# A hybrid encoder layer on one core: first sweep, transposes of the decayed k and the decay inputs one product later, the decays' products directly ahead of those inside the chunk

## The chip, the cores and the metric

The kernel runs on one core of one Trainium2 chip. The metric is the device time of one execution in microseconds (us). The time before is 1314.11 us, the median of three runs (1314.02 to 1314.79).

## What is computed

One layer of an encoder for 2048 tokens of width 1024, in float32. One projection of the input makes the columns of two groups of heads; each group mixes the tokens in its own way; their outputs, put side by side, pass an output projection, and a LayerNorm over the scaled residual ends the layer. The change lies in the first group, gated linear attention in both directions (the reference cut to it):

```python
def gla_chunked(q, k, v, log_a, strict):
    b = jnp.cumsum(gc, axis=3)                 # running sum of the log decays in a chunk
    b_last = b[:, :, :, -1:, :]
    q_dec = qc * jnp.exp(b)
    k_dec = kc * jnp.exp(-b)
    k_tail = kc * jnp.exp(b_last - b)
    attn = jnp.where(mask, jnp.einsum('nbhtd,nbhsd->nbhts', q_dec, k_dec), 0.0)
    o_intra = jnp.einsum('nbhts,nbhsv->nbhtv', attn, vc)
    def step(state, inp):
        o = jnp.einsum('bhtd,bhdv->bhtv', qd, state)
        state = state * jnp.exp(bl)[..., None] + jnp.einsum('bhsd,bhsv->bhdv', kt, vv)
        return state, o

log_af = jax.nn.log_sigmoid(lr_f @ wg2_f + bg_f) / GLA_TAU     # lr: 16 columns of the projection
o = rms_norm(gla_chunked(q, k, v, log_af) + flip(gla_chunked(flip(q), flip(k), flip(v), flip(log_ab))))
```

The second group is latent attention with a softmax and rotary position tables (cos and sin of position times frequency). Those tables are computed by VectorE during the first sweep too, and for that reason they matter here.

## The kernel before, in words

Every large product is done in three matmuls (`mm3`, L420, L421, L422): each float32 operand is split into a rounded high part and a low rest, and high·high, low·high and high·low are added up. ScalarE writes the high part (`hi`, L366), and VectorE or GpSimd subtracts it to give the low one (`lo`, L372). So most tiles come as pairs: `xah`/`xal` (input), `kh`/`kl`, `qbh`/`qbl`, `kth`/`ktl`, `Ah`/`Al`.

The first sweep (`sweep_a`, L603) goes over 16 chunks of 128 tokens, from the last to the first: i = 0 to 15, chunk c = 15 - i. Steps 1 to 3 follow an order written out by hand (`ORDER_A`). Steps 4 to 15 are made by the callback `step(i, STEPS_A)`, with one period of about 22.5 us. In each, TensorE runs four groups of eight products over the model width: `ipa_0` (288 columns: q and the decay inputs lr), `ipa_1` (384: k and the first part of v), `ipa_2` (384: the rest of v) and the gate `ipg` (512). Between them stand the small products of the linear attention. `STEPS_A` says after which product of which group each stands; "cur" is for the step's own chunk, "prev" for the chunk before:

- after product 4 of `ipa_0`: transposes of q and k of the previous chunk (`qT`, `kT`), from which VectorE makes `qd` (L937) and `kd` (L956) with the decay factors E;
- after product 3 of `ipa_1`: `kt` (L970), four transposes of the decayed k of the previous chunk, and `lrT` (L870), one transpose of this chunk's decay inputs, which VectorE writes as `lr`. ScalarE copies them to `kth` and `lrTs`;
- after product 5 of `ipa_1`: `z` (L882), the decays' products, four matmuls from `lrTs`. With them come, in program order, ScalarE's Abs, Exp and Ln (L886, L888, L890) and VectorE's `za` (L892), two scans (L903, L905), the chunk sums `cl` and E (L915); `zdone` names the instruction of L915. `cw` (L925) is issued with `z`;
- after product 7 of `ipa_1`: `Ap` (`ga_intra`), the products inside the previous chunk. ScalarE copies one half to `At` (L987), VectorE fills the other in by a mask (L989), then `Ah` and `Al` (L372);
- after product 3 of `ipa_2`: `Up`, the state's products; then `Us` by VectorE (L1028) and four GpSimd instructions (L1030 on `Us`, L1036 and L1055 on `Sb`, L1051 on `Sm`);
- after product 3 of `ipg`: `Op`, then `oi` (L1008, L1010).

A group's results leave PSUM right after its last product, ahead of what `STEPS_A` puts there: ScalarE's `k` and high part of `VV` after `ipa_1`. After `ipg` the gate is made in `gs` by three ScalarE instructions and one of VectorE (`silu`, L1477 to L1483).

Two PSUM buffers serve `ipa_0`, `ipa_1`, `ipa_2` and `ipg` in turn, so a step's `ipa_1` writes where the `ipg` of the step before stood, and its first weight load waits until VectorE's `gs` (L1483) has read that. GpSimd also makes `xal` (L372, 128x1024), the low part of a later chunk's input, once ScalarE has written `xah`; `xah` waits for the last matmul that reads the buffer, in `ipg`.

The position tables' angles come in parts (`rope_angles`, L558 to L598), one part in each of the steps 4 to 8, ordered behind that step's `zdone`. Steps 5, 6 and 7 each have a rounding (L566 and L567) and three L570 instructions; step 5 has L580 too, and step 7 begins with L590.

Engines run their own instructions in the program's order, and a scheduler makes that order from dependencies and estimated times; so a later `z` also moves instructions of ScalarE and VectorE.

Of the kernel before, what the change touches and what calls it, by code (L numbers as in the profile page):

```python
# [56 lines left out]
av.2 av.2 gs.3 cw.3 gs.3  # L57
"""

STEPS_A = {(0, 4): [("q", "prev"), ("k", "prev")], (1, 3): [("kt", "prev"), ("lrT", "cur")],  # L60
           (1, 5): [("z", "cur"), ("cw", "cur")], (1, 7): [("intra", "prev")], (2, 3): [("state", "prev")],
           (3, 3): [("av", "prev")]}
ENGINES = tuple(getattr(mybir.EngineType, n) for n in ("PE", "Activation", "DVE", "Pool", "SP"))
LATE_ORDER = ENGINES[1], ENGINES[3], ENGINES[4]
RND = 1.5 * 2.0 ** 23
# [290 lines left out]
class K:  # L356
# [25 lines left out]
    def in_order(self, last, engines=None):  # L382
# [6 lines left out]
        for i in traced[n:]:  # L389
            if i.engine in (engines or ENGINES):  # L390
                if i.engine in last:
# [219 lines left out]
    def sweep_a(self):  # L611
        tc, nc, ins, cp = self.tc, self.nc, self.ins, self.cp
        with ExitStack() as ctx:
# [26 lines left out]
            with tc.tile_pool(name="sta", bufs=1, reuse_waits="tile") as sta:  # L640
# [5 lines left out]
                for g, (c0, n) in enumerate(A_GROUPS):  # L646
                    k = 0
# [30 lines left out]
            def step(i, steps):  # L678

                def after(g, k):  # L680
                    for n, d in steps.get((g, k), ()):
                        run(n, i if d == "cur" else i - 1)
                for g in range(3):
                    for k in self.products(ch[i], g, after):
                        pass
                    after(g, NK - 1)
                if i and ch[i]["c"] not in LATE_GATES:
                    for k in self.gate_products(ch[i]["c"], *ch[i]["x"], ip):
                        after(3, k)
                    self.gate_end(ch[i]["c"], g1)  # L690
# [9 lines left out]
            for t in ORDER_A.split():  # L700
                n, i = t.split(".")
# [6 lines left out]
            for i in range(4, NCH):  # L708
                c = ch[i]["c"]
                if c > 0:  # L710
                    for f in (self.ga_ld, self.ga_x):
                        for _ in f(i + 1):
                            pass
                else:
                    self.xlate = [self.split_x(xp, self.load_x(NCH - 1, "xb"), NCH - 1, "xb")]
                    self.xraw = self.load_x(NCH - 2, "xb")
                step(i, STEPS_A)
                if i < 4 + 5:
                    with self.after(ch[i]["zdone"]):
                        next(rope)  # L720
                if i == 9:
                    self.rope_tables(hpi)
            i = NCH - 1
# [335 lines left out]
    def late_gates(self):  # L1059
# [23 lines left out]
        with self.part("wz"):  # L1083
            self.Wz = next(wz)
        self.tail = {e: self.merge(e, names) for e, names in zip(ENGINES[1:], (TAIL_ACT, TAIL_DVE))}

# [922 lines left out]
```

## Time and profile before

| | |
|---|---|
| median of three runs | 1314.11 us (1314.02 to 1314.79) |
| the profiled execution's own time | 1313.98 us |
| its span in the profile | 1312.0 us |
| TensorE busy | 1288.9 us of the span (98%) |
| VectorE, ScalarE, GpSimd busy | 963.2, 812.9, 785.0 us |
| `kt` of step 4 and of step 15 start at | 91.73 and 339.49 us of the span |

In the profile's rows PE is TensorE's matmul, PEld its weight load (which may run beside the matmul ahead of it), DVE is VectorE, ACT ScalarE and POOL GpSimd. A row of the timeline has the start in us from the span's start, the duration in us, engine, line, operation, the tile written and the tiles read, sizes, and how many instructions of one kind were put together (x4). In brackets stands how long the engine was idle before it, and what ended that. Matmuls overlap, so what one costs is read from the distance between starts. A row of the waits has the waiting engine, tile and line, what it waited for, the sum in us, the times, and the longest.

### The profile page before, as it was taken

Reading aid. Unit: us, or ns where it says so; the run is one execution under the profiler, and the core shown is the slowest. Engines: PE = TensorE matmul, PEld = TensorE weight load, DVE = VectorE, ACT = ScalarE, POOL = GpSimd, SP = SyncE. Lnnn points to the kernel's source line nnn. Section 1 sums busy time; section 2 is a strip of 40 time slices with the busy share of each in tenths; the row PEclk is TensorE's granted clock in tenths of the full one; section 3 lists DMA queues with packets and bytes.
Section 4 is the critical chain, followed back from the end, with each engine's and each line's share of the span. In section 5 each row is a group of like instructions: output and inputs, shape, how many; then the busy total and the mean of one; then the engine's idle time right before and its main releaser. Section 6 shows DMA issues by size and latency. Waiting matters only on the chain.

```text
span 1312.0 us, 19984 instructions
## 1 busy us (share of the span) xinstructions
PE 1288.9 (98%) x7081; PEld 1130.2 (86%) x7081; DVE 963.2 (73%) x1712; ACT 812.9 (62%) x1339; POOL 785.0 (60%) x494
## 2 busy tenths in 40 slices
PE   7999999999999999999999999999999999999997
PEld 7999999999889999999788888888888887788886
DVE  7967685655675455555888888888888888469997
ACT  6765656555575656664787877888888888511110
POOL 0143333232467666671388888889999999764441
PEclk9999999999999999999999999999999999999999
DMA  8132313132475555655401111122223110576662
GB/s 283 63 99 55 92 53 93 49 80 66 152 245 173 193 192 177 204 198 184 114 1 41 41 42 41 41 57 64 58 70 101 48 41 9 89 234 200 216 193 97
DMA packets 107819, 145.81 MB, mean 111 GB/s; under 512 B 17250, under 2 KB 62694, under 8 KB 107720
## 3 DMA queue, kind: packets, MB, share of 16 engines
q1 hardware_dynamic: 99128, 142.41, 35.3%
q0 software_dynamic: 672, 2.10, 0.4%
q8 instruction: 56, 0.92, 0.3%
q10 hardware_dynamic: 7920, 0.03, 0.3%
q14 instruction: 43, 0.35, 0.2%
HBM read 94.14 MB, written 50.36 MB: 110 GB/s over the span
## 4 chain that ended last, share of the span: by engine, by line
PE 65%; ACT 2%; POOL 1%; DMA 1%; DVE 1%; issue 0%; SPq 0%; DVEq 0%; ACTq 0%; POOLq 0%
PE pS L1521 4%; PE pS L1524 4%; PE pS L1523 4%; PE pS L1525 4%; PE o L420 4%; PE pS L1522 4%; PE o L422 4%; PE o L421 4%; PE po L421 2%; PE po L422 2%; PE po L420 2%; PE pz L421 2%; PE pz L420 2%; PE pz L422 2%; PE ipm L422 2%; PE ipm L420 2%
## 5 line engine op out<-in xcount | busy, mean ns | idle before, releaser
L372 POOL TENSOR_TENSOR pl<-s,ph 128x1024 fp32r<-128x1024 f32 x128 | 306.8, 2411 | 67.0 <-ACT ph L366 61.8
L1543 DVE TENSOR_TENSOR rm<-pS,rm 128x512 f32<-128x512 f32 x210 | 144.9, 690 | 44.2 <-ACT s L1530 39.0
L1530 ACT ACTIVATE s<-pS 128x1024 f32<-128x1024 f32 x128 | 131.4, 1026 | 67.9 <-PE pS L1525 65.9
L1567 DVE TENSOR_TENSOR s<-s,mb 128x1024 f32<-128x1024 f32 x128 | 151.2, 1213 | 9.5 <-PE mb L1561 9.3
L1030 POOL TENSOR_TENSOR Us<-Us,cw 128x512 f32<-128x512 f32 x16 | 18.5, 1157 | 226.7 <-DVE Us L1028 174.9
L366 ACT ACTIVATE ph<-s 128x1024 fp32r<-128x1024 f32 x128 | 135.0, 1056 | 16.7 <-PE o L422 16.1
L1571 ACT ACTIVATE s<-s 128x1024 f32<-128x1024 f32 x128 | 131.4, 1050 | 13.8 <-DVE s L1567 13.7
L420 PE MATMUL ipa<-wah,xah 128*128 128x384 f32 (+1 forms) x384 | 130.9, 341 | 6.1 <-ACT wah L366 5.9
L422 PE MATMUL ipa<-wah,xal 128*128 128x384 f32 (+1 forms) x384 | 125.3, 326 | 0.0
L421 PE MATMUL ipa<-wal,xah 128*128 128x384 f32 (+1 forms) x384 | 124.9, 325 | 0.0
L1521 PE MATMUL pS<-qh,ckvT_h 128*128 128x512 f32 x256 | 103.7, 405 | 0.7 <-ACT s L1571 0.4
L420 PE MATMUL o<-ph,vh 128*128 128x512 f32 x256 | 102.6, 401 | 0.0
L422 PE MATMUL o<-ph,vl 128*128 128x512 f32 x256 | 101.3, 396 | 0.0
L1524 PE MATMUL pS<-rh,krs 128*128 128x512 f32 x256 | 101.2, 395 | 0.0
L421 PE MATMUL o<-pl,vh 128*128 128x512 f32 x256 | 101.1, 395 | 0.0
L1523 PE MATMUL pS<-qh,ckvT_l 128*128 128x512 f32 x256 | 100.9, 394 | 0.0
L1525 PE MATMUL pS<-rl,krs 128*128 128x512 f32 x256 | 100.7, 393 | 0.0
L1522 PE MATMUL pS<-ql,ckvT_h 128*128 128x512 f32 x256 | 100.6, 393 | 0.0
L1594 DVE TENSOR_TENSOR ap<-ap,s 128x512 f32<-128x512 f32 x120 | 83.1, 692 | 7.0 <-ACT s L1571 5.1
L372 POOL TENSOR_TENSOR ol<-of,oh 128x512 fp32r<-128x512 f32 x32 | 43.1, 1347 | 61.5 <-ACT oh L366 61.5
L420 PEld LDWEIGHTS ipa<-wah,xah 128*128 128x128 f32 x384 | 73.6, 192 | 7.2 <-ACT wah L366 6.4
L420 PE MATMUL pz<-xch,wzh 128*128 128x256 f32 x256 | 74.8, 292 | 0.0
(325 smaller groups left out, 3862.0 us busy)
## 6 DMA issues: line engine op xcount, KB each, us to landing
xcf<-xT_dram SPq DMA_DIRECT2D x16, 512.0 KB, 5.1
xr<-x_dram SPq DMA_DIRECT2D x16, 512.0 KB, 5.8
out_dram<-rr SPq DMA_DIRECT2D x32, 256.0 KB, 2.0
xaf<-xT_dram SPq DMA_DIRECT2D x14, 512.0 KB, 4.1
oib<-oi_s SPq DMA_DIRECT2D x16, 256.0 KB, 5.3
qdb<-qd_s SPq DMA_DIRECT2D x16, 256.0 KB, 4.4
SU<-su_s SPq DMA_DIRECT2D x16, 256.0 KB, 4.5
ub<-u_s SPq DMA_DIRECT2D x16, 256.0 KB, 4.8
```

What stands on the lines that cost most here:

```text
L366: return nc.scalar.activation(dst, src, AF.Copy).ins
L372: return e.tensor_tensor(dst, src, hi.bitcast(F32), ALU.subtract).ins
L420: mm(out, ah, bh, start=start, stop=False)
L421: mm(out, ah, bl, start=False, stop=False)
L422: mm(out, al, bh, start=False, stop=stop)
L1521: mm(ps[:, e], kh, qh, start=True, stop=False)
L1522: mm(ps[:, e], kh, ql, start=False, stop=False)
L1523: mm(ps[:, e], kl, qh, start=False, stop=False)
L1524: mm(ps[:, e], kr, rh, start=False, stop=False)
L1525: mm(ps[:, e], kr, rl, start=False, stop=True)
L1543: V.tensor_tensor(d["rm"], src[:, e], d["rm"], ALU.max)
L1567: V.tensor_tensor(s, s, d["mb"][:, None, :].to_broadcast([P, 2, QB]), ALU.subtract)
```

## The change

`kt` and `lrT` go from behind product 3 to behind product 4 of `ipa_1`; `z` and `cw` go from behind product 5 to behind product 7, directly ahead of `intra`. In the last step (c = 0) `z` and `cw` stay one product further ahead, behind product 6.

```diff
-STEPS_A = {(0, 4): [("q", "prev"), ("k", "prev")], (1, 3): [("kt", "prev"), ("lrT", "cur")],
-           (1, 5): [("z", "cur"), ("cw", "cur")], (1, 7): [("intra", "prev")], (2, 3): [("state", "prev")],
+STEPS_A = {(0, 4): [("q", "prev"), ("k", "prev")], (1, 4): [("kt", "prev"), ("lrT", "cur")],
+           (1, 7): [("z", "cur"), ("cw", "cur"), ("intra", "prev")], (2, 3): [("state", "prev")],
            (3, 3): [("av", "prev")]}
+STEPS_A_LAST = {**STEPS_A, (1, 6): [("z", "cur"), ("cw", "cur")], (1, 7): [("intra", "prev")]}
...
-                step(i, STEPS_A)
+                step(i, STEPS_A if c else STEPS_A_LAST)
```

One line more makes every line behind L62 higher by one in the changed kernel.

**Step 5, TensorE.** The rows around the moved products, before; `wah_206` stands for product 3 of `ipa_1`, `wah_208` for product 4, and so on to `wah_214` for product 7:

```order
L422 MATMUL ipa_1_1479<-wah_206,xal_1185 128x384
L970 MATMUL kt_1492<-ident,kd_1459 128x128 x4
L870 MATMUL lrT_1501<-ident,lr_221 98x128
L420 MATMUL ipa_1_1479<-wah_208,xah_1184 128x384
...
L422 MATMUL ipa_1_1479<-wah_210,xal_1185 128x384
L882 MATMUL z_1511<-lrTs_1503,wg 128x128 x4
L420 MATMUL ipa_1_1479<-wah_212,xah_1184 128x384
...
L422 MATMUL ipa_1_1479<-wah_214,xal_1185 128x384
L420 MATMUL Ap_1546<-qbh_222,kh_1461 128x256
```

And now:

```order
L423 MATMUL ipa_1_1479<-wah_208,xal_1185 128x384
L971 MATMUL kt_1495<-ident,kd_1459 128x128 x4
L871 MATMUL lrT_1504<-ident,lr_221 98x128
L421 MATMUL ipa_1_1479<-wah_210,xah_1184 128x384
...
L423 MATMUL ipa_1_1479<-wah_214,xal_1185 128x384
L883 MATMUL z_1522<-lrTs_1506,wg 128x128 x4
L421 MATMUL Ap_1546<-qbh_222,kh_1461 128x256
```

`kt` and `lrT` have moved by one product, `z` by two, and nine matmuls instead of six stand between `lrT` and `z`. It is the same in steps 4 to 9 and 11 to 14. In step 10, where the scheduler puts `lrT` and `z` between the matmuls of `Ap` both before and now, only `kt` moves.

**Step 5, ScalarE.** From the copies of `kt` and `lrT` on, before:

```order
L366 ACTIVATE lrTs_1503<-lrT_1501 98x128
L886 ACTIVATE za_1516<-z_1511 128x512
L888 ACTIVATE za_1516<-za_1516 128x512
L366 ACTIVATE k_10_1541<-ipa_1_1479 128x512
L890 ACTIVATE za_1516<-za_1516 128x512
L366 ACTIVATE VV_1543<-ipa_1_1479 128x128
L987 ACTIVATE At_1559<-Ap_1546 128x512
```

And now:

```order
L367 ACTIVATE lrTs_1506<-lrT_1504 98x128
L367 ACTIVATE k_10_1517<-ipa_1_1479 128x512
L367 ACTIVATE VV_1519<-ipa_1_1479 128x128
L887 ACTIVATE za_1527<-z_1522 128x512
L889 ACTIVATE za_1527<-za_1527 128x512
L891 ACTIVATE za_1527<-za_1527 128x512
L988 ACTIVATE At_1559<-Ap_1546 128x512
```

The copies `k` and `VV` out of PSUM have moved ahead of all three functions of the decays.

**Step 5, VectorE.** From the end of the decays' sums to the last table instruction, before (`sin` and `cos` are the position tables; the GpSimd instruction L1030 is released by the row of `Us`):

```order
L989 COPY_PREDICATED At_1559<-mask,Ap_1546 128x512
L913 TENSOR_TENSOR cl_1524<-cl_1524 128x4
L915 TENSOR_TENSOR E_10_1521<-E_10_1521,cl_1524 128x512
L566 TENSOR_SCALAR sin<-sin 128x16x32
L372 TENSOR_TENSOR Al_1564<-At_1559,Ah_1562 128x512
L1028 TENSOR_TENSOR Us_1588<-Up_1579,Us_1588 128x512
L567 TENSOR_SCALAR sin<-sin 128x16x32
L570 SCALAR_TENSOR_TENSOR sin<-sin 128x16x32
L372 TENSOR_TENSOR VV_1543<-ipa_2_1566,VV_1543 128x3x128
L570 SCALAR_TENSOR_TENSOR sin<-sin 128x16x32
L580 TENSOR_SCALAR cos<-sin 128x512
L570 SCALAR_TENSOR_TENSOR cos<-sin,cos 128x512
```

And now (the masked copy into `At` has gone ahead of the scans, out of this piece):

```order
L373 TENSOR_TENSOR Al_1564<-At_1559,Ah_1562 128x512
L914 TENSOR_TENSOR cl_1535<-cl_1535 128x4
L916 TENSOR_TENSOR E_10_1532<-E_10_1532,cl_1535 128x512
L1029 TENSOR_TENSOR Us_1588<-Up_1579,Us_1588 128x512
L567 TENSOR_SCALAR sin<-sin 128x16x32
L568 TENSOR_SCALAR sin<-sin 128x16x32
L571 SCALAR_TENSOR_TENSOR sin<-sin 128x16x32
L373 TENSOR_TENSOR VV_1519<-ipa_2_1566,VV_1519 128x3x128
L571 SCALAR_TENSOR_TENSOR sin<-sin 128x16x32
L581 TENSOR_SCALAR cos<-sin 128x512
L571 SCALAR_TENSOR_TENSOR cos<-sin,cos 128x512
```

`Us` has moved ahead of the first table instruction; behind it stand six of them where five stood. In step 6 it is the same (without L580).

**Step 7, VectorE.** The same stretch two steps later, which begins with the table instruction L590, before:

```order
L915 TENSOR_TENSOR E_8_2004<-E_8_2004,cl_2007 128x512
L590 TENSOR_TENSOR sin<-sin,cos 128x16x32
L372 TENSOR_TENSOR Al_2047<-At_2042,Ah_2045 128x512
L1028 TENSOR_TENSOR Us_2071<-Up_2062,Us_2071 128x512
L566 TENSOR_SCALAR sin<-sin 128x16x32
L567 TENSOR_SCALAR sin<-sin 128x16x32
L372 TENSOR_TENSOR VV_2026<-ipa_2_2049,VV_2026 128x3x128
L570 SCALAR_TENSOR_TENSOR sin<-sin 128x16x32 x3
```

And now:

```order
L916 TENSOR_TENSOR E_8_2015<-E_8_2015,cl_2018 128x512
L1029 TENSOR_TENSOR Us_2071<-Up_2062,Us_2071 128x512
L591 TENSOR_TENSOR sin<-sin,cos 128x16x32
L567 TENSOR_SCALAR sin<-sin 128x16x32
L373 TENSOR_TENSOR VV_2002<-ipa_2_2049,VV_2002 128x3x128
L568 TENSOR_SCALAR sin<-sin 128x16x32
L571 SCALAR_TENSOR_TENSOR sin<-sin 128x16x32 x3
```

`Us` has moved ahead of L590; six table instructions follow it instead of five.

## Prediction

> **What bounds the kernel now.** I read the busy shares first (TensorE 98%, the table above), then the stretch of the steps that the change touches, then the waits in that stretch. In a row of the windows, the second number is the stretch, the third TensorE's busy time:
>
> ```profile
> 82.00:350.00 268.00, 267.50 (x1685) 251.47 (x1684) 167.98 (x305) 154.13 (x305) 86.53 (x62) 1.00 0.25 72
> ```
>
> TensorE is busy for 267.5 of 268.0 us at the full clock (1.00), with VectorE at 168 and GpSimd at 87. Nothing but TensorE's own stream sets the end here. So the change can gain only where a matmul is held up inside that stream, and can lose only where it makes TensorE wait. Who waits, from 90 to 380 us:
>
> ```profile
> DVE qd L937 <- PE qT L934: 34.0, 11, 3.9
> ...
> PEld lrT L870 <- issue: 2.2, 10, 0.2
> ...
> PEld z L882 <- ACT lrTs L366: 1.7, 10, 0.2
> ```
>
> In ten steps each, the weight loads of `lrT` and `z` wait about 0.2 us: `z` for ScalarE's `lrTs`, and `lrT`, for which the view has no releaser, by its operand for VectorE's `lr`. VectorE on its side stands idle up to 3.9 us ahead of `qd`: that is the cover for anything made later on it. What the two waits cost TensorE is read from distances between starts. First step 5, then step 4, whose `lr` comes early enough, then step 2, whose `lrTs` does:
>
> ```profile
> 113.94 0.60 PE L970 MATMUL kt<-ident,kd 128*128 128x128 f32 x4
> ...
> 114.85 0.34 PE L421 MATMUL ipa<-wal,xah 128*128 128x384 f32 x1
> ...
> 115.74 0.66 PE L882 MATMUL z<-lrTs,wg 98*128 98x128 f32 x4
> 116.24 0.39 PE L420 MATMUL ipa<-wah,xah 128*128 128x384 f32 x1
> ...
> 117.33 0.28 PE L420 MATMUL Ap<-qbh,kh 128*128 128x256 f32 x1
> ```
>
> ```profile
> 91.73 0.60 PE L970 MATMUL kt<-ident,kd 128*128 128x128 f32 x4
> ...
> 92.45 0.33 PE L421 MATMUL ipa<-wal,xah 128*128 128x384 f32 x1
> ```
>
> ```profile
> 56.10 0.56 PE L882 MATMUL z<-lrTs,wg 98*128 98x128 f32 x4
> 56.49 0.45 PE L420 MATMUL ipg<-wgh,xah 128*128 128x512 f32 x1
> ```
>
> From `kt` to the second matmul behind it: 0.91 us in step 5, 0.72 in step 4, so `lrT`'s wait costs 0.19. The block of `z` takes 0.50 against 0.39: 0.11.
>
> **The gain.** One product is three matmuls, 0.52 us, so `lrT` asks for `lr` 0.52 later and `z` for `lrTs` 0.52 more behind `lrT`: both exceed the 0.2 that is missing. That gives 0.30 us a step in steps 5 to 9 and 11 to 14: 9 x 0.30 = 2.7 us. The waits above, 2.2 + 1.7 over ten steps, set the upper end (3.9). Step 4 has no wait to lose but the start of `z` (nothing counted); step 10 keeps `lrT` and `z` inside `Ap` (nothing). In step 15 the tail behind it waits for something else:
>
> ```profile
> 356.95 0.39 PE L422 MATMUL Ap<-qbh,kl 128*128 128x256 f32 x1 [0.34 <-DVE kl L372]
> ```
>
> What `ipa_1` gains there runs into this wait for `kl`, made by VectorE and ScalarE: 0 to 0.3, I take 0.1. **Gain: 2.8 us.** That `z` stands next to `Ap` and not between products costs nothing that I can see: 0.39 to 0.50 bounds it, and its neighbour matmuls are shorter, not longer.
>
> **What comes later.** The decays now go through ScalarE behind `k` and `VV`:
>
> ```profile
> 116.44 0.60 ACT L886 ACTIVATE za<-z 128x512 f32<-128x512 f32 x1 [0.75 <-PE z L882]
> ...
> 117.61 0.58 ACT L366 ACTIVATE k<-ipa 128x512 f32<-128x512 f32 x1
> 118.08 0.62 ACT L890 ACTIVATE za<-za 128x512 f32<-128x512 f32 x1
> 118.61 0.27 ACT L366 ACTIVATE VV<-ipa 128x128 fp32r<-128x128 f32 x1
> 118.96 0.60 ACT L987 ACTIVATE At<-Ap 128x512 f32<-128x512 f32 x1
> ```
>
> `Ap` will start 0.30 earlier, at 117.03, and `z` 0.39 ahead of that, at 116.64. The last matmul of `ipa_1` starts at about 116.47 and `k` 0.4 behind it, at 116.87 (an estimate from the 0.3 that Abs stood behind the start of the last matmul of `z`); then `k` takes 0.47, `VV` 0.35, Abs 0.63, Exp 0.54, so Ln starts at 118.86 where it started at 118.08: +0.78. On VectorE in step 5 (rows of before):
>
> ```profile
> 118.74 0.69 DVE L892 SCALAR_TENSOR_TENSOR za<-z,za 128x512 f32<-128x512 f32 x1 [2.49 <-ACT za L890]
> ...
> 123.26 0.68 DVE L915 TENSOR_TENSOR E<-E,cl 128x512 f32<-128x512 f32 x1
> ...
> 124.80 0.68 DVE L1028 TENSOR_TENSOR Us<-Up,Us 128x512 f32<-128x512 f32 x1
> 125.40 0.42 DVE L567 TENSOR_SCALAR sin<-sin 128x512 f32<-128x512 f32 x1
> 125.85 1.41 DVE L570 SCALAR_TENSOR_TENSOR sin<-sin 128x512 f32<-128x512 f32 x1
> ...
> 128.88 1.26 DVE L580 TENSOR_SCALAR cos<-sin 128x512 f32<-128x512 f32 x1
> 130.17 1.41 DVE L570 SCALAR_TENSOR_TENSOR cos<-sin,cos 128x512 f32<-128x512 f32 x1
> 131.51 0.68 DVE L1010 TENSOR_TENSOR oi<-Op,oi 128x512 f32<-128x512 f32 x1
> 132.90 0.69 DVE L937 SCALAR_TENSOR_TENSOR qd<-qT,E 128x512 f32<-128x512 f32 x1 [0.71 <-PE qT L934]
> 133.51 0.68 DVE L1483 TENSOR_TENSOR gs<-ipg,gs 128x512 f32<-128x512 f32 x1
> ```
>
> By the new order a `VV` (0.2) leaves the stretch from `za` to E and `Al` (0.6) enters it: E at 123.26 + 0.78 - 0.2 + 0.6 = 124.45, `Us` 0.6 behind, at 125.05. In a step without table instructions 0.3 to 1.2 us later costs nothing: 3.9 us of idle ahead of `qd` hide it. It is 0.71 in step 5.
>
> **The cost** is in the table steps, where VectorE and GpSimd take turns. GpSimd in step 5:
>
> ```profile
> 125.56 1.15 POOL L1030 TENSOR_TENSOR Us<-Us,cw 128x512 f32<-128x512 f32 x1 [14.23 <-DVE Us L1028]
> 126.79 1.61 POOL L1036 TENSOR_TENSOR Sb<-Sb,Us 64x512 f32<-64x512 f32 x1
> 128.47 1.38 POOL L1051 TENSOR_TENSOR Sm<-Sb,cw 64x512 f32<-64x512 f32 x1
> 129.93 1.11 POOL L1055 TENSOR_TENSOR Sb<-Sb,cw 64x512 f32<-64x512 f32 x1
> 131.45 2.40 POOL L372 TENSOR_TENSOR xal<-xaf,xah 128x1024 fp32r<-128x1024 f32 x1 [0.41 <-ACT xah L366]
> ```
>
> Compare ends. L567 ends at 125.82, GpSimd's `Us` 0.89 later (126.71); the first L570 0.55 after that (127.26), not 0.69 after its own start; `Sb` 1.14 after it (128.40). `Sm` ends at 129.85, L580 0.29 later (130.14), `Sb` 0.90 later (131.04), the last L570 0.54 later, and `xal` 2.27 after that (133.85). So one works while the other holds still, and whoever waits goes next. [...]
>
> Before, L566 was done ahead of `Us`, and L567 slipped in ahead of GpSimd's first instruction, which starts 0.76 after VectorE's `Us`. Now L566 slips in and L567 comes behind it: one turn more, and the last L570 falls behind `xal`. With the hand-overs above, from `Us` at 125.05: L566 ends 126.07, `Us` of GpSimd 126.96, L567 127.25, `Sb` 128.39, L570 128.94, `Sm` 129.84, L570 130.39, `Sb` 131.29, L580 131.58, `xal` 133.85, L570 134.40. `xal` must be waiting when L580 ends:
>
> ```profile
> 130.25 1.06 ACT L366 ACTIVATE xah<-xaf 128x1024 fp32r<-128x1024 f32 x1 [1.97 <-PE ipg L421]
> ```
>
> `xah` ends at 131.31, now 0.30 earlier, and GpSimd is free at 131.29: 0.3 us to spare. Then `oi` starts at 134.33, `qd` 0.6 later at 134.93. `gs` stands behind `qd`, and TensorE's next `ipa_1` behind `gs`:
>
> ```profile
> 134.32 0.36 PE L420 MATMUL ipa<-wah,xah 128*128 128x384 f32 x1
> ```
>
> This is 1.42 behind `qd` (132.90); so it comes at 136.35, where TensorE would have it at 134.32 - 0.30 = 134.02. **Stall of 2.3 us.** Step 7 begins from its E:
>
> ```profile
> 168.28 0.69 DVE L915 TENSOR_TENSOR E<-E,cl 128x512 f32<-128x512 f32 x1
> ```
>
> ```profile
> 179.35 0.36 PE L420 MATMUL ipa<-wah,xah 128*128 128x384 f32 x1
> ```
>
> E at 169.47, `Us` 170.07, L590 ends 171.36, GpSimd's `Us` 172.26, L566 172.55, `Sb` 173.69, L567 173.98, `Sm` 174.88, L570 175.43, `Sb` 176.33, L570 176.88, `xal` 179.15, L570 179.70; `qd` 180.23, `ipa_1` 181.65 against 179.05: **2.6 us.** Step 6 has one table instruction fewer, so its last L570 still precedes `xal`, ending at 154.34, with `qd` at 154.87:
>
> ```profile
> 155.40 0.69 DVE L937 SCALAR_TENSOR_TENSOR qd<-qT,E 128x512 f32<-128x512 f32 x1 [1.88 <-PE qT L934]
> ```
>
> It is wanted at 155.40 - 0.30 = 155.10: no stall, 0.2 to spare. Steps 4 and 8 have short parts under the full cover. DMAs: only the store of `qd` in the last step changes place; no group here waits for it. Sum: 4.9 - 2.8 = **+2.1 us**. The profiled execution took 1313.98, which gives 1316.1; the median is 0.13 above it, so 1316.2.
>
> **The rivals.**
>
> *The table instruction keeps its turn.* `xal` waits, but the last L570 follows L580 without a gap, and could take the turn first. It would end 0.69 behind L580 (a two-input instruction of its size, as E), at 132.27; `qd` at 132.80, a stall of 0.2; in step 7 177.57, `qd` 178.10, 0.5. Sum 0.7 - 2.8 = -2.1: 1312.0. Against it: at each hand-over of the rows above, the waiting side went next. [...] 0.17.
>
> *All of it is hidden*, since the turns fall otherwise than I draw them (a shorter `xal`, or L567 still ahead of GpSimd): -2.8, 1311.3. Against it: the order puts L567 behind L566, and 0.42 + 0.6 exceeds the 0.76. 0.08.
>
> *Slower: the decays' chain ends later still*, on ScalarE, because `k` and `VV` hold Abs back longer than I took. Each 0.1 us on E adds 0.1 to the stall of step 5 and of step 7, and past 0.2 also to step 6. From 0.3 later on it is slower than before by over 0.2%; at 0.5 the price is 0.5 + 0.5 + 0.3 = 1.3, so 1317.5. For it: `k`'s start is my estimate. Against it: ScalarE is idle ahead of it. 0.16.
>
> *The gain does not come*, because the weight loads' waits only show what TensorE loses anyway; then the stalls stand alone: 1319.0. Against it: steps 4 and 5 differ by just this 0.19. 0.04.
>
> **How the numbers follow.** My forecast, stalls at both steps and the full gain, has 0.55: 1316.2, between 1315.5 and 1316.9 if each stall is off by 0.3. A difference of 0.2%, 2.6 us, is about what a measurement of this kernel can tell from no change: faster is below 1311.5, slower above 1316.7. Slower: 0.16 + 0.04 and the upper end of the forecast, 0.08. Faster: the hidden case, 0.08, and part of the first rival, 0.06. Within: 0.58. The range from 1311.4 to 1317.6 takes in the first rival and the later chain; the forecast alone has 1315.5 to 1316.9.
>
> **What would show it.** Right: the waits of `lrT` and `z` are gone; `kt` to the second matmul behind it is 0.72 and `z` 0.39 in every step; the last L570 of steps 5 and 7 is some 2.8 us long, with `xal` inside it; `ipa_1` at about 136 and 181 us waits for `gs` over 2 us, and nowhere else; a plain step lasts 0.3 less. Wrong: `xal` starting behind the last L570, a stall in step 6 or in a step without table instructions, or `lrT` and `z` at the old distances.

## The result, and the profile after

The changed kernel takes 1318.31 us (median of 11 executions, 1315.94 to 1320.32) against 1314.11 (11, 1313.15 to 1315.55): a ratio of 1.0031 with a 95% interval of 1.0024 to 1.0039, so it is slower, by 0.3%. The profiled execution took 1317.47 us, span 1315.5, which is 3.5 us more than that of before. The forecast was 1316.2 with a range up to 1317.6: the direction holds, the size doesn't.

The waits of the changed kernel from 90 to 380 us, cut to those that answer to the rows shown of before:

```profile
DVE qd L938 <- PE qT L935: 31.2, 9, 3.9
...
PEld ipa L421 <- DVE gs L1484: 4.6, 2, 2.4
...
PE ipa L421 <- DVE gs L1484: 4.1, 2, 2.2
```

The waits of `lrT` and `z` are gone, and a new one is there, twice: TensorE's `ipa_1` for `gs`. Step 5 on TensorE, where both moved products stand:

```profile
114.29 0.60 PE L971 MATMUL kt<-ident,kd 128*128 128x128 f32 x4
...
115.01 0.33 PE L422 MATMUL ipa<-wal,xah 128*128 128x384 f32 x1
```

```profile
116.41 0.56 PE L883 MATMUL z<-lrTs,wg 98*128 98x128 f32 x4
116.81 0.33 PE L421 MATMUL Ap<-qbh,kh 128*128 128x256 f32 x1
```

0.72 us from `kt` to the second matmul behind it, and 0.40 for the block of `z`: both at the values without a wait (0.72 and 0.39). Now VectorE, from the `Us` of step 5 to the instruction that TensorE waits for:

```profile
124.74 0.68 DVE L1029 TENSOR_TENSOR Us<-Up,Us 128x512 f32<-128x512 f32 x1
125.34 0.42 DVE L567 TENSOR_SCALAR sin<-sin 128x512 f32<-128x512 f32 x1
125.79 1.15 DVE L568 TENSOR_SCALAR sin<-sin 128x512 f32<-128x512 f32 x1
126.98 1.67 DVE L571 SCALAR_TENSOR_TENSOR sin<-sin 128x512 f32<-128x512 f32 x1
...
130.01 1.26 DVE L581 TENSOR_SCALAR cos<-sin 128x512 f32<-128x512 f32 x1
131.31 2.77 DVE L571 SCALAR_TENSOR_TENSOR cos<-sin,cos 128x512 f32<-128x512 f32 x1
134.00 0.68 DVE L1011 TENSOR_TENSOR oi<-Op,oi 128x512 f32<-128x512 f32 x1
134.60 0.67 DVE L938 SCALAR_TENSOR_TENSOR qd<-qT,E 128x512 f32<-128x512 f32 x1
135.20 0.67 DVE L1484 TENSOR_TENSOR gs<-ipg,gs 128x512 f32<-128x512 f32 x1
```

and GpSimd's last two instructions there:

```profile
129.62 1.37 POOL L1056 TENSOR_TENSOR Sb<-Sb,cw 64x512 f32<-64x512 f32 x1
131.07 2.46 POOL L373 TENSOR_TENSOR xal<-xaf,xah 128x1024 fp32r<-128x1024 f32 x1
```

This is the forecast turn: the second instruction of the rounding takes 1.15 us instead of 0.42, and the last table instruction 2.77 instead of 1.41, from just before `xal` gets the turn to 0.55 us behind its end (133.53). Then `qd` and `gs` follow without idle time. What was not in the forecast stands on TensorE behind the wait:

```profile
133.70 0.29 PE L423 MATMUL ipa<-wah,xal 128*128 128x288 f32 x1
135.92 0.61 PE L421 MATMUL ipa<-wah,xah 128*128 128x384 f32 x1 [1.93 <-DVE gs L1484]
136.33 0.52 PE L422 MATMUL ipa<-wal,xah 128*128 128x384 f32 x1
136.65 0.52 PE L423 MATMUL ipa<-wah,xal 128*128 128x384 f32 x1
```

After the idle time the matmuls stand 0.32 us apart instead of 0.175. The windows of the same trace show it in the granted clock, the number behind the closing bracket of the fifth engine:

```profile
135.00:139.50 4.50, 3.58 (x11) 3.58 (x12) 3.54 (x7) 2.78 (x6) 0.00 (x0) 0.62 0.79 244
139.50:184.00 44.50, 42.59 (x272) 40.33 (x271) 35.09 (x52) 23.65 (x45) 15.96 (x10) 1.00 0.17 48
184.00:188.00 4.00, 3.71 (x23) 3.68 (x24) 2.91 (x6) 2.78 (x7) 0.00 (x0) 1.00 0.98 279
```

0.62 in the mean behind the first stall, 1.00 behind the second. Laid out by steps, as the distance between the starts of `kt` of one step and of the next (us):

| from step | 5 | 6 | 7 | 8 | 9 | 11 to 14, mean |
|---|---|---|---|---|---|---|
| before | 22.51 | 22.50 | 22.53 | 22.50 | 22.53 | 22.51 |
| after | 25.92 | 22.18 | 24.64 | 22.18 | 22.19 | 22.20 |

From step 10, where `lrT` and `z` stand inside `Ap` in both, it is 22.93 before and 22.92 after. A plain step is 0.32 shorter, step 5 is 3.4 longer, step 7 is 2.1 longer.

### The profile page after: what moved, and what is told of

It is laid out like the page before. It is cut to its first block, busy times and chain, and to the rows that moved or that the text cites. A ratio compares the mean times of both kernels' runs of the same rounds, so it can differ in the third digit from the quotient of the medians.

```text
span 1315.5 us, 19983 instructions
## 1 busy us (share of the span) xinstructions
PE 1287.0 (98%) x7081; PEld 1132.3 (86%) x7081; DVE 967.6 (74%) x1712; ACT 817.8 (62%) x1339; POOL 784.0 (60%) x494
## 4 chain that ended last, share of the span: by engine, by line
PE 85%; DVE 4%; ACT 3%; POOL 2%; issue 1%; DMA 1%; SPq 0%; DVEq 0%; POOLq 0%; ACTq 0%
PE pS L1522 4%; PE pS L1525 4%; PE pS L1524 4%; PE o L421 4%; PE pS L1526 4%; PE pS L1523 4%; PE o L423 4%; PE o L422 4%; PE ipa L421 3%; PE ipa L423 3%; PE ipa L422 3%; PE pz L422 2%; PE pz L421 2%; PE pz L423 2%; PE po L422 2%; PE po L423 2%
```

## The experiments

The theory after the result: the extra turn behind `xal` makes the two stalls, and TensorE's idle time in them halves its clock for some us, in some executions behind one, in others behind both. The rivals: the loss comes from the later decays themselves, from the denser stream on TensorE, or from elsewhere. The experiments were timed beside the kernel before, which took 1316.2 to 1316.8 us (medians) there; so their ratios are compared, not their times.

**Take the stalls away (e1_spread).** The tables' instructions are cut into parts at other places:

```diff
                         invf[:, None, :].to_broadcast([P, NCH, 32]), ALU.mult)
-        yield
...
         nround(big)
+        yield
         take(A, m1)
...
         take(A, p1)
+        yield
         take(A, p2)
         take(A, p3)
-        yield
```

> The change, with the position tables' 22 VectorE instructions cut at other places: 4, 4, 5, 4 and 5 in steps 4 to 8 instead of 2, 6, 5, 6 and 3, so that none falls behind xal. Theory (turns behind xal make the stalls, and the stalls' idle time halves TensorE's granted clock for some us): both stalls and the slow stretch go, only the gain of 0.3 us in nine steps is left: 1311.3 us (1310.5 to 1312.0), clock 1.00 all through steps 4 to 15. Rival 1 (the extra loss beyond the stalls comes from the denser TensorE stream or from the later decays themselves): stalls gone, but 1 to 2 us of loss stay, 1312.5 to 1313.5, with stretches under clock 1.00. Rival 2 (the gain isn't there): 1314.

Ratio 0.9977 (0.9968 to 0.9986), which is 3.0 us of the time before (the medians, 1313.45 and 1316.28, differ by 2.8). Every plain step lasts 22.18 to 22.20 us, steps 5 and 7 too, no matmul of `ipa_1` waits for `gs`, and the clock is 1.00 from 82 to 355 us. The gain is there, and all the loss belonged to the stalls. This is also the best version of the study.

**Only the tables' place (e2_before_us).** The kernel before, with one wait for the order moved:

```diff
-        V.tensor_tensor(Us, Up[:, :, 0], Us, ALU.add)
+        d["usdone"] = V.tensor_tensor(Us, Up[:, :, 0], Us, ALU.add).ins
...
-                    with self.after(ch[i]["zdone"]):
+                    with self.after(ch[i - 1]["usdone"]):
```

> The kernel before, kt, lrT and z at their old places, only the position tables' part of each step ordered behind that step's Us on VectorE, as the change has it. Theory: the same extra turn, so ipa_1 waits for gs by about 2.1 us in step 5 and 2.5 us in step 7, with TensorE's clock halved for about 3 us behind one or both; no gain: 1314.1 + 4.6 + 1.5 to 3 = 1320 to 1322 us. Rival (the stalls come from the decays being 0.8 us later, not from the turns): 1314 to 1315.

Ratio 1.0002 (0.9994 to 1.0011): no loss. The theory's value failed, the rival's came, and the trace says why. VectorE and GpSimd in step 5 of this kernel:

```profile
129.86 1.26 DVE L580 TENSOR_SCALAR cos<-sin 128x512 f32<-128x512 f32 x1
131.16 0.69 DVE L570 SCALAR_TENSOR_TENSOR cos<-sin,cos 128x512 f32<-128x512 f32 x1
```

```profile
131.43 2.68 POOL L372 TENSOR_TENSOR xal<-xaf,xah 128x1024 fp32r<-128x1024 f32 x1 [0.59 <-ACT xah L366]
```

The extra turn is there (L567 takes 1.15 us, as in the change). But GpSimd is idle for 0.59 us, `xah` isn't ready yet, and the last table instruction starts 0.27 us ahead of `xal` and takes 0.69; now `xal` is the one that waits (2.68 instead of 2.40). So the extra turn alone is not enough. It costs only when `xal` already waits as L580 ends. Here `xah` ends at 131.29, 0.17 us behind L580; in the changed kernel it ends at 130.82, 0.45 ahead of L581's end. Counted back from the end of `xah`, `Us` starts 6.69 us ahead of it here and 6.08 in the change: the later decays and the shorter step together make up these 0.61 us. So the rival is half right: without the later decays there is no stall. But they are not enough either, since e1_spread has them and has none.

**Shorten the last turn (e3_xal_halves).**

```diff
-        self.lo(xl[:, :, 0], xf, xh[:, :, 0], "dve" if i < 4 else "pool")
+        if i < 4:
+            self.lo(xl[:, :, 0], xf, xh[:, :, 0], "dve")
+        else:
+            for k in (0, NK // 2):
+                ks = slice(k, k + NK // 2)
+                self.lo(xl[:, ks, 0], xf[:, ks], xh[:, ks, 0], "pool")
```

> The change, with xal of steps 4 on made by two GpSimd instructions of half the size. The last table instruction of steps 5 and 7 then waits for one half only (about 1.1 us less). Theory: stalls of about 1.1 and 1.4 us, too short to lower the clock: 1314.1 - 2.8 + 2.5 = 1313.8 us (1313 to 1314.5), clock 1.00. Rival (any stall of TensorE brings a slow stretch): 1315 to 1317. Rival (both halves go ahead of the table instruction): stalls as in the change, 1318.

Ratio 0.9997 (0.9988 to 1.0006). The waits and the last table instruction of step 5:

```profile
PEld ipa L421 <- DVE gs L1489: 2.4, 2, 1.3
...
PE ipa L421 <- DVE gs L1489: 1.9, 2, 1.1
```

```profile
130.83 1.66 DVE L571 SCALAR_TENSOR_TENSOR cos<-sin,cos 128x512 f32<-128x512 f32 x1
```

Steps 5 and 7 are 1.1 and 1.4 us longer than plain ones, and the clock is 1.00 in both places. A shorter `xal` is a shorter stall, to the tenth that was expected.

**Lengthen it (e4_long).**

```diff
         take(r2, m4)
+        for _ in range(2):
+            take(n, 0.5)
         yield
...
         take(A, p3)
+        for _ in range(2):
+            take(n, 0.5)
         yield
```

> The change, with two more table instructions of the kind L571 (on a scratch tile that is recomputed next) at the end of the parts of steps 5 and 7: adds work that the result doesn't need. Stalls grow by about 1.3 us each, to 3.5 and 3.8 us. Theory (idle time of TensorE halves its clock, the longer the surer): both steps have a slow stretch in every execution, 1318.3 + 2.6 + 0.5 to 2 = 1321.4 to 1323 us. Rival (the slow stretch has nothing to do with the idle time): 1318.3 + 2.6 = 1320.9, slow stretch as rare as in the change.

Ratio 1.0062 (1.0049 to 1.0074), about 8 us over before. The first matmuls of `ipa_1` in steps 6 and 8, and matmuls a little later:

```profile
136.76 0.69 PE L421 MATMUL ipa<-wah,xah 128*128 128x384 f32 x1 [3.38 <-DVE gs L1488]
137.25 0.52 PE L422 MATMUL ipa<-wal,xah 128*128 128x384 f32 x1
```

```profile
186.53 0.44 PE L421 MATMUL ipa<-wah,xah 128*128 128x384 f32 x1 [3.65 <-DVE gs L1488]
186.81 0.34 PE L422 MATMUL ipa<-wal,xah 128*128 128x384 f32 x1
...
188.13 0.52 PE L423 MATMUL ipa<-wah,xal 128*128 128x384 f32 x1
188.45 0.52 PE L421 MATMUL ipa<-wah,xah 128*128 128x384 f32 x1
```

Both stalls have a stretch of slow matmuls here (0.52 us instead of 0.34). The second begins only 1.4 us after TensorE has gone on (187.90 against 186.53): here the clock fell some time behind the end of the idle time. The windows laid out below fit this.

**One part alone (e5_kt_alone and e6_z_alone).** The kernel before with `kt` and `lrT` one product later, and the change with them at the old place:

```diff
-STEPS_A = {(0, 4): [("q", "prev"), ("k", "prev")], (1, 3): [("kt", "prev"), ("lrT", "cur")],
+STEPS_A = {(0, 4): [("q", "prev"), ("k", "prev")], (1, 4): [("kt", "prev"), ("lrT", "cur")],
```

```diff
-STEPS_A = {(0, 4): [("q", "prev"), ("k", "prev")], (1, 4): [("kt", "prev"), ("lrT", "cur")],
+STEPS_A = {(0, 4): [("q", "prev"), ("k", "prev")], (1, 3): [("kt", "prev"), ("lrT", "cur")],
```

> Only kt and lrT one product later, z at its old place. The table instructions keep the order of before. lrT's wait goes (0.19 us a step), but lrTs follows kt's copy kth on ScalarE and so comes 0.52 us later, while z asks 0.19 earlier than before: z waits about 0.8 us instead of 0.11. Theory: 9 steps x (0.8 - 0.11 - 0.19) = 4.5 us slower, ratio about 1.003, no idle of TensorE over 1 us and no slow stretch of its clock. Rival (lrTs was held by lr alone, so half of the gain comes by itself): 1.7 us faster, ratio 0.9987.

Ratio 0.9988 (0.9979 to 0.9996): the rival holds, this half is worth 1.6 us by itself. A plain step is 22.34 us, 0.17 less. ScalarE and the weight load of `z` in step 5:

```profile
114.37 0.60 ACT L366 ACTIVATE q<-ipa 128x512 f32<-128x512 f32 x1 [1.08 <-DVE lr L372]
115.04 0.60 ACT L366 ACTIVATE kth<-kt 128x512 fp32r<-128x512 f32 x1
115.53 0.27 ACT L366 ACTIVATE lrTs<-lrT 98x128 fp32r<-98x128 f32 x1
```

```profile
115.85 0.52 PEld L882 LDWEIGHTS z<-lrTs,wg 98*128 98x128 f32 x4 [0.19 <-ACT lrTs L366]
```

I had `kth` follow `kt`, 0.52 us later. But it stands behind `q` on ScalarE, and `q` waits for `lr`; so `lrTs` is only 0.12 later, and `z` waits as it did.

> Only z and cw moved, kt and lrT at their old place. z's wait goes (0.11 us a step, 1.0 us), lrT's 0.19 stays. The tables' order is that of the change. Theory: xal is ready only 0.1 earlier than before, Us stands where it does in the change, so the last table instruction still falls behind xal in steps 5 and 7: stalls of 2.1 and 2.4 us and a slow stretch behind one or both, - 1.0 + 4.5 + 1.5 to 3 = 5 to 6.5 us slower, ratio 1.004 to 1.005. Rival (the table instruction is in time once xal is 0.2 later, as with the tables alone moved): 1 us faster, ratio 0.999.

Ratio 1.0046 (1.0034 to 1.0058), the theory's value. The wait for `gs` is there twice (4.6 us in all on the weight loads), the wait of `lrT` remains, and a plain step lasts 22.37 to 22.40 us. So the move of `z` alone brings the stalls, and it brings only 0.12 us a step. `xah` ends 0.45 us ahead of L581 here too (130.24 against 130.69), as in the change, though a step is only 0.12 shorter: so most of the 0.61 us comes from the later decays, and not from the shorter step.

**The change twice more (e7_again1, e8_again2).**

> The change itself once more, for its profile. Theory: the stalls of 2.1 and 2.4 us stand in every execution, the stretch at half clock behind them doesn't: behind none, one or both, so that the start of kt in step 15 lies at 341.5, 343 or 344.5 us. Rival (the program alone decides it): at 136 us only, as before, kt at 343.1 us.

> As for e7_again1, a third execution of the change with a profile.

1320.23 and 1318.33 us; the two behave differently. The stretch behind each stall, first in e7_again1, then in e8_again2:

```profile
135.00:139.50 4.50, 4.08 (x17) 3.98 (x18) 3.04 (x6) 2.58 (x6) 0.00 (x0) 0.70 0.88 284
...
184.00:188.00 4.00, 4.00 (x15) 4.00 (x15) 2.42 (x5) 1.98 (x5) 0.00 (x0) 0.57 0.93 259
```

```profile
135.00:139.50 4.50, 3.72 (x23) 3.69 (x24) 3.40 (x7) 3.13 (x7) 0.00 (x0) 1.00 0.88 249
...
184.00:188.00 4.00, 4.00 (x21) 3.96 (x21) 1.25 (x3) 1.31 (x3) 0.00 (x0) 0.74 0.64 224
```

In the one the clock falls behind both stalls, in the other behind the second alone, and in the profile after it was the first alone. The waits are the same in all three (4.6 and 4.1 us). That also gives the price without the clock: 24.37 us for step 5 in e8_again2 and 24.64 for step 7 in the profile after, and 1.55 more where the clock fell (25.92 and 26.19). `kt` of step 15 starts 247.76 us behind that of step 4 before, and 251.00, 252.55 and 250.99 in the three executions of the change.

**Which stall lowers the clock.** The same traces settle this. Behind the stalls the clock stood at half for 3.41 us each time, and the two stretches of e7_again1 begin 47.79 us apart, 14 times as much (at 136.77 and 184.56). So a trace can be laid out in windows of 3.41 us from such a start. In the profile after, these are the window with most of each stall's idle time and the window behind it:

```profile
132.62:136.03 3.41, 1.48 (x12) 1.24 (x10) 3.41 (x5) 0.71 (x3) 0.91 (x1) 1.00 0.15 54
136.03:139.44 3.41, 3.41 (x11) 3.41 (x12) 2.51 (x5) 2.08 (x5) 0.00 (x0) 0.50 0.87 258
180.41:183.82 3.41, 1.68 (x14) 1.44 (x12) 3.41 (x4) 0.47 (x2) 1.48 (x1) 1.00 0.00 0
183.82:187.23 3.41, 2.94 (x17) 2.91 (x18) 3.09 (x6) 2.25 (x6) 0.00 (x0) 1.00 0.95 250
```

Idle time is a window's length less TensorE's busy time. TensorE was idle for 3.41 - 1.48 = 1.93 us of the window ahead of the half clock. The second stall is longer, 2.20 us, but the end of a window cuts it; only 1.73 us fall into one, and the clock stays up. In the same way the first stall of e8_again2 is cut into 1.00 and 0.94 us. Laid out like this from 20 us of the span on, the traces of all thirteen runs give one picture: behind every window with 1.87 us of idle time or more the clock was at half, behind every full-clock window with 1.61 or less it was not, and of the five windows from 1.65 to 1.73 it fell behind one. Where the windows lie against the program differs from trace to trace; so the same stall costs 1.55 us more in one execution and not in another.

**A place that the change doesn't touch.** Far behind the sweep, at about 1140 us, TensorE waits for the tile `wol` in every trace. In e9_before_spread (described next), which has the products at their old places:

```profile
1139.56 0.54 PE L421 MATMUL po<-wol,oh 128*128 128x512 f32 x1 [2.00 <-POOL wol L372]
```

```profile
1139.88:1143.29 3.41, 3.41 (x9) 2.63 (x8) 0.00 (x0) 0.11 (x1) 3.41 (x3) 0.50 0.76 231
```

The wait is 1.40 us in the profile before, 1.51 in the one after and 2.0 in all the experiments, and in seven of the thirteen traces the clock is at half behind it (for 6.83 us in e4_long, for 3.41 in the others), with the changed order and with the old one. So executions with either order can differ by such a stretch, which has nothing to do with the change.

**The tables alone, and a stall in between (e9_before_spread, e10_xal_34).** The first is the kernel before with the new cuts of e1_spread; the second has `xal` in pieces of six and two eighths:

```diff
-            for k in (0, NK // 2):
-                ks = slice(k, k + NK // 2)
+            for ks in (slice(0, 6), slice(6, NK)):
```

> The kernel before with the position tables cut as in e1_spread, nothing else. Theory: the tables cost nothing where no turn falls behind xal, so cutting them anew gains nothing by itself: ratio 1.000 (0.9993 to 1.0007), and e1's gain is that of the moved products alone. Rival (the tables held up the kernel before too): faster by 1 to 3 us, ratio 0.998 to 0.999.

Ratio 0.9997 (0.9988 to 1.0006), steps of 22.51 us: cutting the tables anew gains nothing by itself.

> The change, with xal of steps 4 on in two GpSimd instructions, of three quarters and one quarter. Stalls of about 1.6 and 1.9 us, between those of e3 (1.1 and 1.4, no slow stretch) and of the change (2.2 and 2.5, a slow stretch behind one or both in three profiles). Without a slow stretch: 1.0 us over e3, ratio 1.0004. Theory (a fixed raster of windows judges the idle time): a slow stretch in some executions only, ratio 1.0004 to 1.0016. Rival (a sharp limit over 2 us): none, ratio 1.0004.

Ratio 1.0007 (0.9998 to 1.0016). Steps 5 and 7 are 1.64 and 1.92 us longer than plain ones, and the profile has a clock of 1.00 behind both. Two of the eleven executions stand 1.3 and 2.2 us over the median, which may be a fallen clock or not; no trace shows which. Its longest idle time is 1.67 us, less than the 1.73 that left the clock up twice, and the profile itself has a stretch at half clock at 1141 us, in the place that the change doesn't touch; so these two need not come from the stalls.

**The last step (e11_spread_last_old).** e1_spread with the old places for c = 0:

```diff
-STEPS_A_LAST = {**STEPS_A, (1, 6): [("z", "cur"), ("cw", "cur")], (1, 7): [("intra", "prev")]}
+STEPS_A_LAST = {(0, 4): [("q", "prev"), ("k", "prev")], (1, 3): [("kt", "prev"), ("lrT", "cur")],
+                (1, 5): [("z", "cur"), ("cw", "cur")], (1, 7): [("intra", "prev")], (2, 3): [("state", "prev")],
+                (3, 3): [("av", "prev")]}
```

> e1_spread with the last step (c = 0) at the old places. Theory on the tail: kt of the tail comes 0.35 us later than in e1_spread (the waits of lrT and z are back in step 15), but the Ap matmuls behind it wait for kl alone as before and not for qbl too, 0.5 us less: the tail's second Ap product starts within 0.2 us of e1_spread's, so the last step's gain is given back at once. Rival (the new places gain 0.3 there for good): 0.3 later than in e1_spread.

The tail of e1_spread and of this kernel:

```profile
352.97 0.38 PE L422 MATMUL Ap<-qbl,kh 128*128 128x256 f32 x1 [0.64 <-DVE qbl L373]
```

```profile
353.16 0.38 PE L424 MATMUL Ap<-qbl,kh 128*128 128x256 f32 x1 [0.16 <-DVE qbl L375]
```

This trace runs 0.32 us later already at `kt` of step 14 (314.75 against 314.43). So `Ap` is 0.13 earlier with the old places, by one trace of each: what step 15 gains is given back at once, and about a tenth more.

## Why the prediction was wrong

- **The gain** (2.8 us forecast, of it 2.7 in nine steps at 0.30) is right and a little low: 0.32 to 0.33 a step, 2.98 us from step 4 to step 15 in e1_spread (244.78 against 247.76), and 3.0 us by its ratio.
- **The last step** (+0.1) is wrong in sign: `Ap` waits for `qbl` in the tail, and about 0.1 us is lost (e11_spread_last_old, one trace).
- **The later chain.** `Us` was forecast at 125.05 and came at 124.74, in a trace that runs 0.17 us ahead there. It costs nothing in plain steps, and step 6 has no stall (22.18 us), as forecast.
- **The stalls** (2.3 and 2.6 forecast) measure 2.19 and 2.46 where the clock stays up. Their mechanism was as the prediction put it, down to `xal` waiting when L580 ends; e2, e3 and e6 bear it out, and e2 shows that this condition decides. The first rival (the table instruction keeps its turn) falls: in the change the instruction ends 0.55 us behind `xal`; it goes first only in e2, where `xah` is late.
- **What failed is the sum, in the step "+2.1 us".** It took a stall to cost its own length, and put at nothing what TensorE's idle time does to TensorE's clock. Each stall can bring a stretch of 3.41 us at half clock, which costs 1.55 us more: no term of the sum and no rival had it. From 1313.98, with - 2.98 + 4.65 and the tail's 0.1, comes 1315.8 us without it, 1317.3 with one and 1318.9 with two. The profiled execution, with its single stretch, took 1317.47; the executions lie between 1315.94 and 1320.32 with the median at 1318.31, and the lowest is within 0.3 us of what was forecast. No trace says how many stretches the others had. Four of the eleven lie above 1318.9, by up to 1.4 us; executions of the kernel before lie up to 1.4 over their median as well, and the place at 1140 us can add a stretch, so these four are not accounted for one by one.
- **The other rivals.** *The gain does not come* gave 1319.0, near the measured median, and is wrong all the same: a plain step is 0.32 us shorter. *The chain ends later still* gave 1317.5 and falls too: `Us` came no later than forecast, and step 6 has no stall. *All of it is hidden* falls with the two stalls.

What stays open: the exact share of a window that lowers the clock, between 1.61 and 1.87 us of idle time in 3.41, and whether anything besides TensorE's idle time counts. Of the eight stalls in four traces with waits of 2.2 and 2.4 us (the profile after, e6, e7, e8), five lowered the clock; the stalls of e3 and e10, with waits of up to 1.3 and 1.9, did not in one profile each.

## What to carry to other kernels

A stall of the engine that bounds a kernel is not priced by its length alone: look at the granted clock behind it, and in several executions, since the same stall may lower the clock in one and not in the next (here step 5 took 25.92 us in the profile after and 24.37 in e8_again2). Before a move, see which pair of engines that take turns (here VectorE and GpSimd) the moved work passes, count the turns left after it and ask whether the long instruction of the other engine will already be waiting at the last turn; six tenths of a us decided 2 us here. When a move that gains 0.3 us a step brings such a loss, mend what makes the loss (here the cut of the tables), and the gain is to be had.

## What the runs showed of the hardware

TensorE's granted clock fell to half for 3.41 us behind stalls with 2.2 and 2.4 us of waiting weight loads, in some executions of the same program and not in others (five of eight stalls in the profile after, e6_z_alone, e7_again1 and e8_again2): in every case seen where 1.87 us or more of idle time fell into one window of 3.41 us, with the windows laid out from the start of a stretch at half clock. It can begin after TensorE has gone on (1.4 us later in e4_long), so the slow rows need not touch the stall. A DVE table instruction that waits for its turn is shown as busy for up to 2.77 us (the last one of step 5 in the profile after) where it takes 0.69 when it goes first (e2_before_us); GpSimd's `xal` likewise, 2.68 in e2_before_us instead of 2.40 before.
